# Gate and up projections of four feed-forward blocks computed with seven block products for eight (Strassen's scheme in Winograd's form)

## The chip, the core and the metric

The kernel runs on one core of one Trainium2 chip. The metric is device time in microseconds (us). A profiled execution gives the trace; its span is a little shorter than the device time of the same run.

## What is computed

The trunk has two layers on a sequence of 512 frames with a model width of 1024. Each layer is a feed-forward block, a token mixer (layer 0 a hybrid of two attentions, layer 1 a latent attention) and a second feed-forward block; so there are four feed-forward blocks of the same shape, cut from the reference here:

```python
def _swiglu(u, w_gate, w_up, w_down):          # 1024 -> 2816 -> 1024
    return (jax.nn.silu(u @ w_gate) * (u @ w_up)) @ w_down
# per layer, with shift, scale and gate from cond @ ada_w[i] (1024 x 9*1024) + ada_b[i]
u = _rmsnorm(h, norm_g[i, 0]) * (1 + sc1) + sh1
h = h + 0.5 * g1 * _swiglu(u, w_gate[i, 0], w_up[i, 0], w_down[i, 0])
u = _rmsnorm(h, norm_g[i, 1]) * (1 + sc2) + sh2
h = h + g2 * mixer(u)
u = _rmsnorm(h, norm_g[i, 2]) * (1 + sc3) + sh3
h = h + 0.5 * g3 * _swiglu(u, w_gate[i, 1], w_up[i, 1], w_down[i, 1])
```

Everything is float32.

## The kernel before

**Products.** The model dimension lies on 8 blocks (k) of 128 partitions, the 2816 hidden features on 22 tiles (j) of 128; the 512 frames are the columns. A float32 operand is split into a high part and a rest (`split`, L348; for weights `wsplit`, L262), and one float32 product is three matmuls with the smaller types, high by high, high by rest, rest by high (`mm3`, L297, the matmuls on L299 to L301). A weight chunk (`wchunk`) is a DMA of 512 KB into a `raw` buffer, a copy on ACT into `wh` (L265) and a subtraction on DVE into `wl` (L266, operands `raw` and `wh`, both in SBUF). There are two `raw` buffers and four each of `wh` and `wl`.

**A feed-forward block** (`ffn`, L542). For a hidden tile j, `unit` runs 8 x 3 matmuls of 512 columns for the gate and as many for up, into two PSUM tiles (`pj`, `s`); `gated` applies Silu on ACT, multiplies on DVE (L557, one operand in PSUM) and splits the product (L349 on ACT, L350 on DVE). In the three later blocks the first two tiles are computed in two halves of 256 columns, so that they can begin while the normalised input of the second half is still made (`affine`, L411: L413 reads `h` in SBUF and a PSUM tile, L418 two SBUF tiles). The first block has `first_feed` instead, which feeds tiles 0 to 2 block by block of k while its input arrives. After all 22 tiles `back_proj` computes the down projection, 8 x 22 x 3 matmuls, and adds into `h` (L441, in `Back.tile`).

**Work in the background.** The shift, scale and gate vectors need the product of the conditioning vector with `ada_w`. It is cut into items (`ada_chunk`, L182): a DMA of 512 KB into one of two `wide` buffers (L185, from SP) and one DVE instruction over 128 x 1024 that sums along the free axis (L186, both inputs in SBUF). They lie in the list `pending`; `background(n)` issues n of them, and `need` issues one after another until the vector asked for is there.

**Order.** The instructions of each engine are put in order when the kernel is built; each engine runs its list strictly in that order and waits for semaphores of others. GpSimd (POOL) has work in the hybrid mixer only: weight subtractions, rotary products (L656 to L658) and MEMSETs.

The places that the change touches are `ffn`, `u_next` (L604), `affine` and `apply`, `turn_x` of the first feed, and the loop over the layers.

Of the kernel before, what the change touches and what calls it, by code (L numbers as in the profile page):

```python
# [16 lines left out]
P = 128  # L17
NT = 5
NRAW = 2
# [77 lines left out]
def kernel(ctx: ExitStack, tc: tile.TileContext, d):  # L97
# [84 lines left out]

    def ada_chunk(l, j, k, raw=None):
# [62 lines left out]
    def wload(ap, n):  # L246
        raw = wp.tile([P, 1024], F32, tag="raw", name=nm("raw"), bufs=NRAW)
        nc.sync.dma_start(raw[:, :n], ap)
        return raw
# [161 lines left out]
    def affine(src, rb, k, a, b, oh, ol):  # L411
        t = t_tile()[:, :src.shape[-1]]
# [10 lines left out]
    def apply(srcs, rb, c0, c1, a, b, outs):  # L423
        w = c1 - c0
        for k, (src, (oh, ol)) in enumerate(zip(srcs, outs)):
            affine(src[:, c0:c1], rb[:, :w], k, a, b, oh[:, c0:c1], ol[:, c0:c1])
# [115 lines left out]
    def ffn(l, f, u, gate, nxt, feed=None, rate=2, after=None):  # L542
# [22 lines left out]

        if feed is not None:
# [9 lines left out]
            for j in range(3):  # L576
                gated(j, *pss[j], 0, T)
        else:
            j0 = 2
            first = [load(0), load(1)]  # L580
            for c0, c1 in HALVES:
# [3 lines left out]
                for j in range(2):  # L585
                    pss = pj_ps(), s_ps()
                    run_tiles([ps[:, :w] for ps in pss], first[j], u, c0, c1)
                    gated(j, *pss, c0, c1)
        for j in range(j0, NF):
            unit(j, *load(j), 0, T)  # L590
            background(rate)
            if after is not None and j == after[0]:
                after[1]()

        def down(k):
            out = []
            for c, (k0, k1) in enumerate(((0, 8), (8, 16), (16, 22))):
                wh, wl = wchunk(d["wd"][l, f, k][:, k0 * P:k1 * P], (k1 - k0) * P)
                out.append((wh, wl, k1 - k0))
            return out  # L600

        back_proj(gate(), down, hidden, nxt, 1)

    def u_next(l, sub):  # L604
        outs = [(u_tile(), u_tile()) for _ in range(KD)]

        def nxt(acc, c0, c1):
# [8 lines left out]
            def two():  # L616
                with tc.high_priority(offset=PRIO), tc.issue_after(last_mm[0]):
                    rb = spread(dg[0], c1 - c0)
                apply(h_tiles(), rb, c0, c1, acol[l, sub], bcol[l, sub], outs)
            later(HOLD1, one)  # L620
            later(HOLD2, two)
        return outs, nxt
# [580 lines left out]
    def first_ada(k):  # L1203
        for i, j in enumerate((1, 0)):
            n = 2 * k + i
            with tc.issue_after(last_y[0]) if last_y[0] is not None else nullcontext():
                ada_chunk(0, j, k, None if n % 3 == 2 else spare[(n - n // 3) % 4])
# [19 lines left out]
    turned = []  # L1227
# [8 lines left out]
    def first_feed(k):  # L1236
# [8 lines left out]
        t = t_tile()  # L1245
        S.activation(t, turned[k], AF.Identity, scale=acol[0, 0][:, k:k + 1], bias=bcol[0, 0][:, k:k + 1])
        split(*u[k], t)
        if k + 2 < KD:
# [4 lines left out]
    pending.extend(ada_work(0, [("g", 0), ("n", 1), ("g", 1), ("n", 2), ("g", 2)]))  # L1253
# [13 lines left out]

    for l in range(2):
        n_u, n_nxt = u_next(l, 1)
        ffn(l, 0, u, need(gcol, (l, 0)), n_nxt, first_feed if l == 0 else None, 3,  # L1270
# [119 lines left out]
```

## Time and profile before

| | before |
|---|---|
| device time, median of 3 runs | 2006.46 us (2005.85 to 2012.56) |
| device time of the profiled run | 2006.17 us |
| its span | 2004.4 us |
| granted TensorE clock, mean over the span | 0.995 |
| PE busy (matmul) | 1956.1 us, 98% of the span |
| DVE / ACT / POOL busy | 1094.6 / 744.7 / 120.4 us |

"Busy" is the time in which an engine has an instruction in work. Successive matmuls overlap, so their distance is read from starts, not from durations. A granted clock of 1.00 is 2.4 GHz, 0.50 is 1.2 GHz.

### The profile page before, as it was taken

How to read it: one execution, taken by the hardware profiler on the slowest of the kernel's cores; microseconds unless marked ns; L12 is line 12 of the kernel's file. 1: busy time of each engine (PE TensorE's matmuls, PEld its weight loads, DVE VectorE, ACT ScalarE, POOL GpSimd, SP SyncE). 2: the span in 40 equal slices, each digit the busy share in tenths (PEclk: the TensorE clock that was granted, in tenths of full speed). 3: DMA queues.
4: the chain of work that ended last, by engine and by line, in shares of the span. 5: the costliest groups of instructions: out<-in, count | busy, mean ns of one | idle time of the engine just before them, and what ended most of it. 6: DMA issues, size and time to landing. Idle time of an engine off the chain costs nothing.

```text
span 2004.4 us, 25366 instructions
## 1 busy us (share of the span) xinstructions
PE 1956.1 (98%) x9988; PEld 1652.8 (82%) x9988; DVE 1094.6 (55%) x1893; ACT 744.7 (37%) x1232; POOL 120.4 (6%) x116
## 2 busy tenths in 40 slices
PE   7999999999989999999999999999999999999997
PEld 4888888987878888888889888888988898888886
DVE  7466673479946577777336433323586573333234
ACT  6322222246667442222224233222357543232221
POOL 0000000045553000000000000000000000000000
PEclk9999999999999999999999999999999999999998
DMA  9467773232222238887432333233232023322331
GB/s 334 135 228 241 236 234 105 92 107 67 85 79 80 85 121 270 280 274 248 117 97 85 107 99 95 92 98 97 71 99 71 23 94 109 103 95 95 95 97 61
DMA packets 78412, 260.53 MB, mean 130 GB/s; under 512 B 9426, under 2 KB 12498, under 8 KB 78292
## 3 DMA queue, kind: packets, MB, share of 16 engines
q1 hardware_dynamic: 75892, 254.65, 39.5%
q0 software_dynamic: 1664, 3.28, 0.7%
q8 instruction: 78, 1.28, 0.3%
q10 hardware_dynamic: 736, 0.98, 0.2%
q14 instruction: 42, 0.34, 0.1%
HBM read 249.17 MB, written 2.10 MB: 125 GB/s over the span
## 4 chain that ended last, share of the span: by engine, by line
PE 83%; DVE 10%; ACT 3%; DMA 2%; issue 1%; POOL 1%; SPq 0%; DVEq 0%; ACTq 0%; POOLq 0%
PE pj L299 18%; PE pj L301 18%; PE pj L300 18%; PE s L301 9%; PE s L300 9%; PE s L299 9%; DVE hid L978 1%; DVE m L977 1%; DVE wl L266 1%; DVE hid L767 1%; DVE hid L350 1%; DVE sm L699 1%; PE aux L718 1%; ACT wide L707 1%; ACT wh L265 1%
## 5 line engine op out<-in xcount | busy, mean ns | idle before, releaser
L265 ACT ACTIVATE wh<-raw 128x1024 fp32r<-128x1024 f32 (+1 forms) x331 | 340.8, 1030 | 899.6 <-PE pj L300 561.9
L266 DVE TENSOR_TENSOR wl<-raw,wh 128x1024 fp32r<-128x1024 f32 (+2 forms) x308 | 364.6, 1184 | 417.5 <-ACT wh L265 417.0
L299 PE MATMUL pj<-u,wh 128*128 128x512 f32 (+1 forms) x1035 | 391.1, 379 | 2.0 <-ACT u L349 0.9
L301 PE MATMUL pj<-u,wl 128*128 128x512 f32 (+1 forms) x1035 | 382.5, 370 | 0.7 <-DVE wl L266 0.5
L300 PE MATMUL pj<-u,wh 128*128 128x512 f32 (+1 forms) x1035 | 381.4, 370 | 0.8 <-DVE u L350 0.8
L299 PE MATMUL pj<-hid,wh 128*128 128x512 f32 (+1 forms) x876 | 319.5, 365 | 0.2 <-DVE h L441 0.2
L300 PE MATMUL pj<-hid,wh 128*128 128x512 f32 (+1 forms) x876 | 317.2, 362 | 0.0
L301 PE MATMUL pj<-hid,wl 128*128 128x512 f32 (+1 forms) x876 | 317.2, 362 | 0.0
L301 PE MATMUL s<-u,wl 128*128 128x512 f32 (+1 forms) x841 | 311.3, 370 | 0.0
L300 PE MATMUL s<-u,wh 128*128 128x512 f32 (+1 forms) x841 | 310.8, 370 | 0.0
L299 PE MATMUL s<-u,wh 128*128 128x512 f32 (+1 forms) x841 | 310.6, 370 | 0.0
L299 PEld LDWEIGHTS pj<-u,wh 128*128 128x128 f32 x1035 | 196.3, 190 | 35.6 <-issue 3.1
L301 PEld LDWEIGHTS pj<-u,wl 128*128 128x128 f32 x1035 | 195.5, 189 | 34.4 <-DVE wl L266 1.5
L300 PEld LDWEIGHTS pj<-u,wh 128*128 128x128 f32 x1035 | 195.6, 189 | 31.2 <-DVE u L350 1.9
L186 DVE SCALAR_TENSOR_TENSOR wide<-wide,cond 128x1024 f32<-128x1024 f32 x133 | 161.3, 1223 | 73.4 <-DMA wide<-in_ada 73.2
L299 PEld LDWEIGHTS pj<-hid,wh 128*128 128x128 f32 x876 | 165.5, 189 | 25.8 <-DVE hid L770 0.4
L301 PEld LDWEIGHTS pj<-hid,wl 128*128 128x128 f32 x876 | 165.3, 189 | 25.4
L300 PEld LDWEIGHTS pj<-hid,wh 128*128 128x128 f32 x876 | 165.4, 189 | 24.9
L301 PEld LDWEIGHTS s<-u,wl 128*128 128x128 f32 x841 | 158.8, 189 | 26.8
L300 PEld LDWEIGHTS s<-u,wh 128*128 128x128 f32 x841 | 158.6, 189 | 26.5
L299 PEld LDWEIGHTS s<-u,wh 128*128 128x128 f32 x841 | 158.5, 189 | 26.0
L557 DVE TENSOR_TENSOR t<-t,s 128x512 f32<-128x512 f32 (+1 forms) x93 | 60.5, 651 | 162.8 <-PE s L301 159.5
(214 smaller groups left out, 1920.2 us busy)
## 6 DMA issues: line engine op xcount, KB each, us to landing
raw<-in_wgu SPq DMA_DIRECT2D x176, 512.0 KB, 3.5
wide<-in_ada SPq DMA_DIRECT2D x133, 512.0 KB, 4.4
raw<-in_wd SPq DMA_DIRECT2D x64, 512.0 KB, 3.5
raw<-in_wd SPq DMA_DIRECT2D x32, 384.0 KB, 3.1
raw<-in_hin SPq DMA_DIRECT2D x19, 512.0 KB, 3.5
h<-in_ada SPq DMA_DIRECT2D x11, 512.0 KB, 7.1
raw<-in_hv SPq DMA_DIRECT2D x8, 512.0 KB, 3.5
raw<-in_hout SPq DMA_DIRECT2D x8, 512.0 KB, 3.6
```

Of the source, the lines that this page charges most:

```text
L186: V.scalar_tensor_tensor(raw, raw, 1.0, cond[0], op0=ALU.mult, op1=ALU.mult, accum_out=mod[l][:, j, k:k + 1])
L265: S.activation(wh[:, :n], raw[:, :n], AF.Copy)
L266: (by or V).tensor_tensor(wl[:, :n], raw[:, :n], wh[:, :n].bitcast(F32), op=ALU.subtract)
L299: PE.matmul(ps, ah, bh, start=start, stop=False)
L300: PE.matmul(ps, ah, bl, start=False, stop=False)
L301: last_mm[0] = PE.matmul(ps, al, bh, start=False, stop=stop).ins
L350: return V.tensor_tensor(ol, raw, oh.bitcast(F32), op=ALU.subtract)
L557: V.tensor_tensor(sg[:, :w], sg[:, :w], pu[:, :w], op=ALU.mult)
L699: V.tensor_reduce(nmx, ps[:, :n], axis=AX.X, op=ALU.max, negate=True)
L707: S.activation(pr[qt], pr[qt], AF.Copy, scale=rinv[:, qt:qt + 1])
L718: last_mm[0] = PE.transpose(ps[:, c:c + P], pr[qt][:, kt * P:(kt + 1) * P], ident).ins
L767: V.tensor_tensor(ol, ps, oh.bitcast(F32), op=ALU.subtract)
```

## The change

Two neighbouring hidden tiles are taken as a pair. Their weights are a 2 x 2 arrangement of blocks (two halves of the model dimension by two hidden tiles), and so is the input (two halves of the model dimension by two halves of the frames); four 128-row blocks each stand in a half. For each of gate and up, seven products of 4 x 3 matmuls of 256 columns are made (84 matmuls; the two units that a pair replaces have 48 matmuls of 512 columns for each of gate and up). The products use sums of weight blocks and of input blocks, and their results are recombined. Tiles that stay in the old form: the first four of the first block, the first two of the others. That leaves 9 + 10 + 10 + 10 = 39 pairs, 78 sets of seven products.

- `Forms` holds one set of weights and goes in six steps: four loads of 256 KB; four sums on POOL (L586 to L589, 128 x 512 each); three splits of 1024 columns and one of 512 (ACT L268, DVE L269). `pair_products` calls the steps for the next sets at fixed places between the products of the present one.
- Recombination per set: ACT copies two PSUM halves, DVE adds (L642, L648, L654: one operand in SBUF, one in PSUM), POOL adds 128 x 256 (L649). Per pair: two Silu on ACT, two products on POOL (L696, 128 x 512), four hidden splits of 256 columns (ACT L352, DVE L353).
- Input sums: `input_sums` makes, for each of four pairs of input blocks, four POOL instructions of 256 columns (L559 to L562) and two splits of 512. In the three later blocks the normalised tile is kept without its shift (`kept`), and a POOL TENSOR_SCALAR of 512 columns for each of eight tiles (L782) adds the shift first.
- The down projection is made in three parts after hidden tiles 6, 14 and 22; the first two parts add into `h` by L752, the last runs through `back_proj`. The sets of the next part are brought up to their first splits during the last four k of a part.
- Background: one item for each pair, two for each k of the first two parts; `need` for the gate vector comes after the first part's pairs, no longer after the last tile. `raw` gets four buffers.

```diff
-NRAW = 2
+NRAW = 4
+    def input_sums(t1, t2):
+        lo, hi = slice(0, HALF), slice(HALF, T)
+        G.tensor_tensor(t1[:, lo], t1[:, hi], t1[:, lo], op=ALU.subtract)
+        G.tensor_tensor(t1[:, hi], t1[:, hi], t2[:, hi], op=ALU.add)
+        G.tensor_tensor(t2[:, hi], t2[:, hi], t1[:, lo], op=ALU.add)
+        G.tensor_tensor(t2[:, lo], t2[:, lo], t2[:, hi], op=ALU.subtract)
+        out = []
+        for t in (t1, t2):
+            o = hid_tile(), hid_tile()
+            split(*o, t)
...
+    class Forms:
...
+        def load(self):
+            self.r.append(raw_tile())
+            self.a2 = hid_tile(F32), hid_tile(F32)
+            for i, o in enumerate((self.r[0][:, :T], self.r[0][:, T:], *self.a2)):
+                nc.sync.dma_start(o, self.ap[i])
+
+        def sums(self):
...
+            G.tensor_tensor(s3, a21, a11, op=ALU.subtract)
+            G.tensor_tensor(s2, a22, s3, op=ALU.subtract)
+            G.tensor_tensor(s1, a21, a22, op=ALU.subtract)
+            G.tensor_tensor(s4, a12, s2, op=ALU.subtract)
+
+        def split(self):
+            n = len(self.w)
+            self.w.append(wsplit(self.r[n], 2 * T) if n < 3 else wsplit(self.a2[1], T))
...
+    def pair_products(w, u, sums, nxt):
...
+        ahead(0, 2)
+        w.to(6)
...
+        product(b1[:, lo], "A11", block(0, lo))
+        S.activation(t[:, lo], b1[:, lo], AF.Copy)
+        product(b26[:, lo], "A12", block(1, lo))
+        ahead(0, 3)
+        product(b26[:, hi], "S2", lambda q: sums[q][1])
+        V.tensor_tensor(two(ca), twice(t[:, lo]), two(b26), op=ALU.add)
+        product(b57[:, lo], "S1", lambda q: sums[q][0])
+        ahead(0, 4)
+        ahead(1, 1)
+        product(b57[:, hi], "S3", lambda q: sums[q][2])
+        S.activation(t[:, hi], b57[:, lo], AF.Copy)
+        V.tensor_tensor(two(cb), twice(ca[:, hi]), two(b57), op=ALU.add)
+        G.tensor_tensor(ca[:, hi], cb[:, hi], t[:, hi], op=ALU.add)
+        product(b34[:, lo], "S4", block(1, hi))
+        ahead(0, 5)
+        product(b34[:, hi], "A22", lambda q: sums[q][3])
+        ahead(0, 6)
+        V.tensor_tensor(cb, cb, b34, op=ALU.add)
+        return ca, cb
+    PARTS = ((0, 6), (6, 14), (14, 22))
...
+            for x in g:
+                S.activation(x, x, AF.Silu)
+            left[0] -= 1
+            p = products()
+            for x, y in zip(p, g):
+                G.tensor_tensor(x, x, y, op=ALU.mult)
...
-        for j in range(j0, NF):
-            unit(j, *load(j), 0, T)
-            background(rate)
...
+            g = gate()
+            if p1 < NF:
+                for k in range(KD):
+                    ps = pj_ps()
+                    run_tile(ps, down(k), act, 0, T)
+                    mark[0] = V.scalar_tensor_tensor(h[:, k], ps, g[:, k:k + 1], h[:, k],
+                                                     op0=ALU.mult, op1=ALU.add).ins
+                    background(rate[1])
+                    if k >= KD - 4:
+                        forms[0].to((1, 2, 3, 4)[k - KD + 4])
+            else:
+                back_proj(g, down, act, nxt, 3)
...
+                if keep and c1 == T:
+                    for q in range(KD // 2):
+                        for k in (2 * q, 2 * q + 1):
+                            G.tensor_scalar(kept[k], kept[k], bcol[l, sub][:, k:k + 1], None, op0=ALU.add)
+                        sums.append(input_sums(kept[2 * q], kept[2 * q + 1]))
```

The first place to look at is a pair in the middle of a part. On DVE, of the changed kernel, from the second set of one pair to the first set of the next (in the first block; `wl` are weight splits, `s` and `aux` PSUM tiles, `wide` a background item):

```order
L269 TENSOR_TENSOR wl_1977<-raw_1881,wh_1976 128x1024 [waits DMAHW6_49,DMAHW7_49,PE_49,Activation_49]
L642 TENSOR_TENSOR hid_1948<-t_1950,s_1945 128x512 [waits PE_49]
L269 TENSOR_TENSOR wl_2006<-raw_1938,wh_2005 128x1024 [waits PE_49,Activation_49]
L648 TENSOR_TENSOR hid_1949<-hid_1948,aux_1946 128x512 [waits DVE_49,Activation_49]
L654 TENSOR_TENSOR hid_1949<-hid_1949,aux_1947 128x512 [waits PE_49,Pool_49]
L269 TENSOR_TENSOR wl_2060<-hid_1883,wh_2059 128x512 [waits DMAHW2_49,Activation_49]
L353 TENSOR_TENSOR hid_2067<-hid_1948,hid_2066 128x256 [waits Pool_49]
L353 TENSOR_TENSOR hid_2073<-hid_1948,hid_2072 128x256 [waits DMAHW0_49,Activation_49]
L189 SCALAR_TENSOR_TENSOR wide_2078,mod_92<-wide_2078,cond_94 128x1024
L269 TENSOR_TENSOR wl_2120<-raw_2009,wh_2119 128x1024 [waits DMAHW3_49,DMAHW4_49,PE_49,Activation_49]
```

The splits of the pair's hidden tiles wait for POOL's products, and behind them on DVE stands the first weight split of the next pair's second set. On POOL, which had nothing in a feed-forward block, the same pair in the changed kernel reads:

```order
L586 TENSOR_TENSOR raw_2082<-hid_2010,raw_2009 128x512
L587 TENSOR_TENSOR raw_2081<-hid_2011,raw_2082 128x512
L649 TENSOR_TENSOR hid_1948<-hid_1949,t_1950 128x256
L588 TENSOR_TENSOR raw_2081<-hid_2010,hid_2011 128x512
L696 TENSOR_TENSOR hid_1948<-hid_1948,hid_1820 128x512
L589 TENSOR_TENSOR raw_2082<-raw_2009,raw_2081 128x512
L696 TENSOR_TENSOR hid_1949<-hid_1949,hid_1821 128x512
```

The sums for the set after the next stand ahead of and between the products on which the hidden splits wait.

The second place is the entry of a later feed-forward block (here the second of layer 0), on POOL of the changed kernel; `hid_7601` to `hid_7608` are the kept tiles, `raw_7943` and `raw_7944` hold the sums of the block's first set:

```order
L782 TENSOR_SCALAR hid_7601<-hid_7601,b_2_3707 128x512
L559 TENSOR_TENSOR hid_7601<-hid_7601 128x256
L560 TENSOR_TENSOR hid_7601<-hid_7601,hid_7602 128x256
L561 TENSOR_TENSOR hid_7602<-hid_7602,hid_7601 128x256
L562 TENSOR_TENSOR hid_7602<-hid_7602 128x256
L561 TENSOR_TENSOR hid_7608<-hid_7608,hid_7607 128x256
L562 TENSOR_TENSOR hid_7608<-hid_7608 128x256
L586 TENSOR_TENSOR raw_7944<-hid_7937,raw_7936 128x512
L587 TENSOR_TENSOR raw_7943<-hid_7938,raw_7944 128x512
```

All 24 instructions on the input stand ahead of the first weight sum; the third product of the first pair needs both.

The third place is the down projection of the first part in the first block, on DVE, where before a hidden tile of a unit stood between background items:

```order
L186 SCALAR_TENSOR_TENSOR wide_838,mod_92<-wide_838,cond_94 128x1024
L186 SCALAR_TENSOR_TENSOR wide_841,mod_92<-wide_841,cond_94 128x1024
L266 TENSOR_TENSOR wl_1009<-raw_1006,wh_1008 128x1024
L557 TENSOR_TENSOR t_909<-t_909,s_884 128x512
L350 TENSOR_TENSOR hid_913<-t_909,hid_912 128x512
```

In the changed kernel, from the last items before the gate vector `g_0` to the third k:

```order
L189 SCALAR_TENSOR_TENSOR wide_962,mod_92<-wide_962,cond_94 128x1024 [waits DMAHW6_49,DVE_49]
L189 SCALAR_TENSOR_TENSOR wide_965,mod_92<-wide_965,cond_94 128x1024 [waits DMAHW7_49,DVE_49]
L211 TENSOR_TENSOR g_0_968<-mod_92,vec 128x8 [waits DVE_49]
L213 TENSOR_SCALAR g_0_968<-g_0_968 128x8 [waits DVE_49]
L752 SCALAR_TENSOR_TENSOR h<-pj_971,g_0_968,h 128x512 [waits DVE_49]
L189 SCALAR_TENSOR_TENSOR wide_997,mod_92<-wide_997,cond_94 128x1024 [waits DMAHW0_49]
L752 SCALAR_TENSOR_TENSOR h<-pj_1003,g_0_968,h 128x512
L189 SCALAR_TENSOR_TENSOR wide_1000,mod_92<-wide_1000,cond_94 128x1024 [waits DMAHW1_49]
L189 SCALAR_TENSOR_TENSOR wide_1029,mod_92<-wide_1029,cond_94 128x1024 [waits DMAHW2_49,DVE_49]
L752 SCALAR_TENSOR_TENSOR h<-pj_1035,g_0_968,h 128x512 [waits PE_49]
```

Eight items stand ahead of `g_0`, and each L752 frees one of the two PSUM tiles `pj` for a later k only after the items in front of it.

## Rows read from the trace of the kernel before

**Rows 1.** The page, busy time of each engine (share of the span), instructions.
```profile
PE 1956.1 (98%) x9988; PEld 1652.8 (82%) x9988; DVE 1094.6 (55%) x1893; ACT 744.7 (37%) x1232; POOL 120.4 (6%) x116
```
**Rows 2.** The page, the chain that ended last, by engine.
```profile
PE 83%; DVE 10%; ACT 3%; DMA 2%; issue 1%; POOL 1%; SPq 0%; DVEq 0%; ACTq 0%; POOLq 0%
```
**Rows 3.** Window inside a feed-forward block: engines' busy time, clock, DMA share, GB/s.
```profile
1100.00:1320.00 220.00, 220.00 (x973) 182.16 (x972) 82.39 (x93) 64.47 (x83) 0.00 (x0) 1.00 0.31 98
```
**Rows 4.** Timeline, PE, 512 columns: start, duration, instruction; 46 steps apart.
```profile
1109.64 0.39 PE L300 MATMUL s<-u,wh 128*128 128x512 f32 x1
...
1120.07 0.39 PE L301 MATMUL pj<-u,wl 128*128 128x512 f32 x1
```
**Rows 5.** Timeline, PE, 256 columns; 83 steps apart.
```profile
372.46 0.28 PE L299 MATMUL pj<-hid,wh 128*128 128x256 f32 x1
...
382.41 0.28 PE L301 MATMUL pj<-hid,wl 128*128 128x256 f32 x1
```
**Rows 6.** Groups by line, weight loads of that stretch: busy, mean ns.
```profile
L299 PEld LDWEIGHTS pj<-hid,wh 128*128 128x128 f32 x28 | 5.4, 192 | 0.0
```
**Rows 7.** Groups by line and form: busy us, mean ns, idle before.
```profile
L266 DVE TENSOR_TENSOR wl<-raw,wh 128x1024 fp32r<-128x1024 f32 x268 | 328.0, 1224 | 306.9 <-ACT wh L265 306.4
L266 POOL TENSOR_TENSOR wl<-raw,wh 128x1024 fp32r<-128x1024 f32 x23 | 56.0, 2439 | 96.7 <-ACT wh L265 90.3 <-PE aux L718 6.4
L871 POOL MEMSET hid<- 64x512 f32 x8 | 4.3, 539 | 0.4
```
**Rows 8.** Timeline, POOL, two products of 512 columns in a row.
```profile
534.89 1.29 POOL L656 TENSOR_TENSOR hid<-hid,rope 128x512 f32<-128x512 f32 x1
536.13 1.29 POOL L657 TENSOR_TENSOR hid<-hid,rope 128x512 f32<-128x512 f32 x1
```
**Rows 9.** Timeline, DVE and POOL at the same time in the hybrid mixer.
```profile
417.47 3.25 DVE L350 TENSOR_TENSOR hid<-hid,hid 64x512 fp32r<-64x512 f32 x1
417.79 2.38 POOL L266 TENSOR_TENSOR wl<-raw,wh 128x1024 fp32r<-128x1024 f32 x1
...
423.74 2.92 POOL L266 TENSOR_TENSOR wl<-raw,wh 128x1024 fp32r<-128x1024 f32 x1 [3.57 <-ACT wh L265]
423.77 0.68 DVE L658 TENSOR_TENSOR hid<-hid,t 128x512 f32<-128x512 f32 x1
...
431.50 2.40 POOL L266 TENSOR_TENSOR wl<-raw,wh 128x1024 fp32r<-128x1024 f32 x1 [0.35 <-ACT wh L265]
431.57 2.37 DVE L941 TENSOR_TENSOR hid<-hid 128x32 f32<-128x32 f32 x1
```
**Rows 10.** Timeline, DVE beside POOL, one operand of DVE in PSUM.
```profile
497.38 4.74 POOL L266 TENSOR_TENSOR wl<-raw,wh 128x1024 fp32r<-128x1024 f32 x2 [9.21 <-ACT wh L265]
...
499.70 0.68 DVE L767 TENSOR_TENSOR hid<-pj,hid 128x512 fp32r<-128x512 f32 x1
```
**Rows 11.** Windows after a wait of PE, columns as in rows 3.
```profile
588.00:592.00 4.00, 1.30 (x5) 1.14 (x6) 3.25 (x6) 3.55 (x7) 1.85 (x3) 0.50 0.30 68
592.00:596.00 4.00, 4.00 (x14) 3.04 (x13) 0.85 (x2) 0.77 (x3) 3.21 (x3) 0.71 0.46 168
```
**Rows 12.** Timeline, PE, the end of that wait.
```profile
590.70 0.55 PE L294 MATMUL s<-hid,hid 128*128 128x256 f32 x1 [5.46 <-DMA hid<-hid]
```
**Rows 13.** Timeline, entry of a feed-forward block, DVE.
```profile
1079.48 0.48 DVE L413 SCALAR_TENSOR_TENSOR t<-h,a,aux 128x256 f32<-128x256 f32 x1 [0.34 <-PE aux L403]
...
1086.06 0.47 DVE L418 SCALAR_TENSOR_TENSOR u<-t,b,u 128x256 fp32r<-128x256 f32 x1
```
**Rows 14.** Timeline, same entry, PE: the first matmul of 512 columns.
```profile
1093.07 0.40 PE L299 MATMUL pj<-u,wh 128*128 128x512 f32 x1
```
**Rows 15.** Timeline, DVE: the first two and the 71st of 72 background items.
```profile
742.39 1.22 DVE L186 SCALAR_TENSOR_TENSOR wide<-wide,cond 128x1024 f32<-128x1024 f32 x1
...
743.53 1.22 DVE L186 SCALAR_TENSOR_TENSOR wide<-wide,cond 128x1024 f32<-128x1024 f32 x1
...
944.77 1.23 DVE L186 SCALAR_TENSOR_TENSOR wide<-wide,cond 128x1024 f32<-128x1024 f32 x1 [1.61 <-DMA wide<-in_ada]
```

More of the change, by code (lines that the diff above doesn't have):

```diff
@@ L181, with raw_tile @@
     mark = [None]
+    def raw_tile():
+        return wp.tile([P, 1024], F32, tag="raw", name=nm("raw"), bufs=NRAW)
     def ada_chunk(l, j, k, raw=None):
@@ L246, in wload @@
     def wload(ap, n):
-        raw = wp.tile([P, 1024], F32, tag="raw", name=nm("raw"), bufs=NRAW)
+        raw = raw_tile()
         nc.sync.dma_start(raw[:, :n], ap)
@@ L540, in first_products @@
             mm3(ps, wh[:, sl], wl[:, sl], *u[k], k == 0, k == KD - 1)
-    def ffn(l, f, u, gate, nxt, feed=None, rate=2, after=None):
+    HALF = T // 2
+    def input_sums(t1, t2):
[8 more added lines that the diff above has]
+            split(*o, t)
+            out += [tuple(x[:, c] for x in o) for c in (lo, hi)]
+        return [out[0], out[3], out[1], out[2]]
@@ L543, in ffn @@
+    PARTS = ((0, 6), (6, 14), (14, 22))
+    def ffn(l, f, u, sums, gate, nxt, feed=None, rate=(2, 2), after=None):
         hidden = []
@@ L577, in ffn @@
                 gated(j, *pss[j], 0, T)
+            forms[0].to(2)
+            unit(j0, *load(j0), 0, T)
+            j0 = 4
         else:
@@ L585, in ffn @@
                 for j in range(2):
+                    if c0:
+                        forms[0].to(2 + 2 * j)
                     pss = pj_ps(), s_ps()
@@ L588, in ffn, with down, u_next @@
                     gated(j, *pss, c0, c1)
-        for j in range(j0, NF):
-            unit(j, *load(j), 0, T)
-            background(rate)
[L592 to L604, printed above, removed]
+        for p0, p1 in PARTS:
+            js = range(max(j0, p0), p1, 2)
+            left[0] = 2 * len(js)
+            for j in js:
+                pair(j)
+            if after is not None and p1 == NF:
+                after()
+            act = hidden[p0:p1]
+            def down(k):
+                return [(*wchunk(d["wd"][l, f, k][:, p0 * P:p1 * P], (p1 - p0) * P), p1 - p0)]
+            g = gate()
[10 more added lines that the diff above has]
+                back_proj(g, down, act, nxt, 3)
+    def u_next(l, sub, keep=False):
         outs = [(u_tile(), u_tile()) for _ in range(KD)]
+        kept, sums = [], []
         def nxt(acc, c0, c1):
@@ L1292, in final @@
                     nc.sync.dma_start(d["out"][:, 4 * g:4 * g + 4, c0:c1], o)
-            ffn(1, 1, u, need(gcol, (1, 2)), final)
+            ffn(1, 1, *x, need(gcol, (1, 2)), final)
 def _consts():
```

100 lines of the change are left out of this document (80 added, 20 removed).

## The prediction

> **What bounds the kernel now.** I read the page first: matmuls are in work for 98% of the span, DVE for 55%, POOL for 6% [rows 1]. The chain of waits gives the same order, 83% on PE [rows 2]. Then the windows: inside a feed-forward block PE is busy for the whole of 220 us at full clock, while DVE is busy 37% of it and POOL not at all [rows 3]. So the time of these blocks is the number of matmuls times their pitch. The timeline of PE gives the pitch: 46 steps of 512 columns in 10.43 us, 0.2267 each [rows 4]; 83 steps of 256 columns in 9.95 us, 0.120 each [rows 5]. Two of the half-width matmuls cost 6% more than one of full width.
>
> **Matmuls.** A set (gate or up of a pair) was 48 x 0.2267 = 10.88 us and becomes 84 x 0.120 = 10.08 us. That is 0.80 less, not the eighth that the count of products suggests. For 78 sets: **-62.4 us**. A pair goes from 21.76 to 20.16 us. The down projection has the same matmuls as before, and the pieces of it are priced at nothing in PE time.
>
> **The pairs.** What decides is whether 20.16 us hide the work of the other engines. Two things there are new to a feed-forward block: POOL is used, and DVE's operands lie in SBUF. In the timeline of the hybrid mixer the two engines stop each other. A DVE instruction over 64 x 512 with two operands in SBUF takes 3.25 us and ends when POOL's instruction beside it has ended; one of 32 columns takes 2.37 us beside POOL's 2.40; and POOL's takes 2.92 instead of 2.40 where DVE had begun first [rows 9]. With one operand in PSUM, DVE's instruction takes 0.68 us in the middle of POOL's work [rows 10]. So DVE's instructions with two SBUF operands and POOL's instructions use one thing in turn, each for the whole of an instruction; I call it the port.
>
> Port work of one pair:
> - POOL: eight sums and two products of 512 columns and two adds of 256. Two products in a row start 1.24 us apart and take 1.29 [rows 8]; I take 1.27. For 256 columns a line through this and the 2.44 of 1024 columns [rows 7] gives about 0.68. 10 x 1.27 + 2 x 0.68 = 14.1 us.
> - DVE with two SBUF operands: six weight splits of 1024 columns, two of 512 and four hidden splits of 256. Instructions of 1024 in a row start 1.14 us apart [rows 15], and the mean duration of a split is 1.22 [rows 7]. With 1.14, and 0.6 and 0.35 by columns: 6 x 1.14 + 2 x 0.6 + 4 x 0.35 = 9.4 us. A background item, where one is left, adds 1.14.
> - Sum 23.5 us, or 24.7 with an item: more than the 20.16 of the matmuls, and more than the 21.76 of before.
> - DVE's six recombinations with a PSUM operand, 6 x 0.6 = 3.6 us, run beside POOL. If all fell where POOL is idle, the pair would be 27.1 to 28.3 us. POOL works some 57% of the pair, so I let 1.5 of the 3.6 stand alone: 24.1 + 1.5 = **25.6 us**, 5.4 over the matmuls. The order supports that this isn't hidden: behind POOL's products stand the hidden splits on DVE, and behind these the next set's first weight split.
>
> The first set of a part has its sums and splits (4 x 1.27 + 4.0 = 9.1 us) under the down projection of the part before. Two pairs at a part's start are therefore 2 x 25.6 - 9.1 = 42.1 us against 40.3, 1.8 late. In 12 parts there are 39 pairs, so 27 passages from a pair to the next: 11 first ones at 1.8 and 16 others at 5.4: **+106 us**. Bounds: 16 at 3.3 (port alone) and nothing for the first, 53; all serial, 16 x 8.1 + 11 x 4 = 174.
>
> **The clock.** After PE had waited 5.46 us [rows 12], the next two windows show granted clocks of 0.50 and 0.71 [rows 11]: 6 to 7 us at 1.2 GHz, which costs half of that, 3.4 us. In a pair the 5.4 us of waiting fall in several pieces, so I take about a third of that, 1.25, for each of the 16 passages: **+20** (0 to 27).
>
> **The entry of the three later blocks.** Take T0 as the first normalised tile of the second half. Before, PE has its two halved tiles done and begins at full width at T0+13.6 [rows 13, 14]. The third product of the first pair (S2, after two of 12 x 0.12) is due at T0+16.4. Its weights pass POOL behind all 24 instructions on the input. Eight TENSOR_SCALARs of 512: the trace has none on POOL; its nearest rows are a MEMSET of 512 on half the partitions, 0.54 [rows 7], and the two-input product, 1.27. I take 0.9, the middle. 8 x 0.9 + 16 x 0.68 + 3 x 1.27 = 21.9 us. DVE's own port work in that time (eight additions in the normalisation [rows 13], eight splits of 512 of the sums, weight and hidden splits) is about 10 us and takes turns with it. With the first tile's 0.9 and the split on ACT and DVE behind the sum, S2 is ready at about T0+35.7: 19.3 us late, three times 58, between 49 and 67 by the two prices of the TENSOR_SCALAR. Each such wait costs the 3.4 of the clock besides: **+68 us** (59 to 77). The Trainium skill, page "GPSIMD Engine Reference", section "4.1 Engine selection", says that one-input operations there run at about the rate of its lanes; an estimate by that page, 512 columns at 1.2 GHz or 0.43 us, would make each entry 3.8 us shorter, 11 in all, and no row of this case shows it.
>
> **The gate vector and the background items.** Before, `need` for the gate came after 22 tiles, with all items long done. Now it comes after the first part, and two items are issued with each k of the down projection; each adds into `h` behind them on DVE, and frees the PSUM tile that a later k waits for. A run of items goes at 2.89 us each (70 steps in 202.4 us), held by its DMA, although DVE needs 1.14 [rows 15]. In the first block 16 such items lie between the first part's last pair and the sixth addition, and the first product of the next pair waits for a tile freed there: 16 x 2.89 + 3.7 = 50 us where the part's down projection (8 x 18 x 0.2267) takes 32.6: 17 to 20 late. In the second block of layer 0, 15 items: 14 to 17. In layer 1 the items are fewer than the k can carry or used up: nothing. Together 34, with the clock twice: **+41 us** (30 to 45).
>
> **The rest.** The first feed gains 16 POOL instructions of 256 and eight splits of 512, 16 x 0.68 + 8 x 0.6 = 15.7 us of port work; the last quarter of it, 3.9, can't be hidden: +5 (0 to 10). Ends of the parts, where hidden splits wait for POOL: +3 (0 to 10). The mixers get four `raw` buffers; I cost that at nothing, covered by their matmuls (-5 to 5).
>
> **Sum.** -62 + 106 + 20 + 68 + 41 + 5 + 3 = +181 us. On the profiled run's 2006.2 us that is 2187, and the run lies 0.3 below the median shown; I take **2185 us**. With all low ends -62 + 53 + 59 + 30 - 5 = +75, 2081; with all high ends 2292.
>
> **Rivals.**
> 1. *Matmuls alone.* Everything new hides under PE: 2006 - 62 = 1944 us. For it: DVE is free 63% of the time in these blocks [rows 3]. Against: 23.5 us of port work in 20.16. It ends on the other side, and the point from which it decides is a port pair under 20.2 us, that is POOL's 512 columns at 0.9 us or less. Chance 0.06.
> 2. *No port, only queues.* If DVE and POOL ran freely, DVE would need 14 and POOL 14 us for a pair, and pairs would hide. What stays is POOL's list at the entry (9.3 late, 28 for three), the items (41) and some 8 of the rest: 2006 - 62 + 77 = 2021; with easier entries it comes to no change. Against: each overlap in [rows 9]. Chance 0.07.
> 3. *The port stays with one side.* DVE's instruction that found POOL at work waited for all of it, and POOL's 2.92 came after two DVE instructions in a row [rows 9]. If the waiting side loses several turns, a pair is all serial, 28.3 us, and PE waits long enough for the low clock in each: the high end, 2280. Chance 0.17.
> 4. *Weight loads set the pitch.* A load takes 192 ns [rows 6], as the matmul of 256 columns now comes every 120. If loads didn't overlap each other, a set would be 84 x 0.192 = 16.1 us, 5.2 more than before: +409 for 78 sets, 2415 us, with the port's work hidden under it. Against: the pitch of 0.120 was measured with those loads [rows 5]. Chance 0.02. The page "TensorE: Matmul & The Clock Gate" of the Trainium skill, section "Back-to-back issue gap", says that load and matmul together set the spacing of a stream; at this width the trace shows a spacing by columns alone (0.120 for 256, 0.2267 for 512).
>
> **Chances.** Forecast 0.68. Its own range is 2120 to 2245, the bounds of the pairs' and the entries' terms taken not all to one side. Rival 3 lies above, rival 2 below; 2070 to 2280 leaves out rival 1, rival 4 and part of 2 and 3. Within 0.5% (about what can be told from no change here) is 1996 to 2016: rival 2 with cheap entries, 0.03. Faster: rival 1, 0.06. Slower: 0.91.
>
> **What would show it.** In the timeline after: POOL's sums longer than 1.29 us or DVE's splits longer than 1.22 where they overlap; pairs 25 us apart in a part's middle, with PE's longest waits on `wl` L269 and behind L353. In the second, third and fourth block PE waits 15 to 22 us before the third product of the first pair, released by DVE `wl` behind POOL L782 and L559 to L562. In the first part's down projection of both blocks of layer 0, PE waits for L752 behind L189. If pairs stand 20 us apart, the port's term is wrong; if PE is idle nowhere in the entry, the entry's.

## Result, and the profile after

The changed kernel takes 2257.98 us (median of 4 runs, 2254.0 to 2264.77) against 2007.36 us of the kernel before: ratio 1.1247, 95% interval 1.1209 to 1.1285. 2185 us was predicted, with 2120 to 2245 as the forecast's own range and 2070 to 2280 as the wider one, which takes in part of rivals 2 and 3; the result lies in the wider one only. The profiled run's span is 2262.8 us.

The first part of the page after, to be held against [rows 1]:

```profile
PE 2016.5 (89%) x12813; PEld 1816.9 (80%) x12820; DVE 1571.1 (69%) x2395; ACT 941.5 (42%) x1662; POOL 919.9 (41%) x672
```

POOL now works 919.9 us, and no engine fills the span: PE has lost nine points of its share. The durations say why. Groups by line and form of the kernel after, busy us and mean ns of one, idle time before:

```profile
L269 DVE TENSOR_TENSOR wl<-raw,wh 128x1024 fp32r<-128x1024 f32 x346 | 489.4, 1415 | 106.4 <-ACT wh L268 104.1
L353 DVE TENSOR_TENSOR hid<-hid,hid 128x256 fp32r<-128x256 f32 x156 | 93.3, 649 | 14.3 <-ACT hid L352 14.3
L586 POOL TENSOR_TENSOR raw<-hid,raw 128x512 f32<-128x512 f32 x78 | 121.1, 1552 | 355.8 <-DVE wl L269 218.2 <-DMA hid<-in_wgs 67.1 <-DMA wide<-in_ada 38.6
L649 POOL TENSOR_TENSOR hid<-hid,t 128x256 f32<-128x256 f32 x78 | 113.2, 1452 | 221.0 <-DVE hid L648 203.1 <-DMA hid<-in_wgs 17.9
L642 DVE TENSOR_TENSOR hid<-t,s 128x512 f32<-128x512 f32 x78 | 52.9, 678 | 0.0
L782 POOL TENSOR_SCALAR hid<-hid,b 128x512 f32<-128x512 f32 x24 | 45.5, 1901 | 402.0 <-DVE u L421 402.0
```

A weight split takes 1415 ns on average where it took 1224 [rows 7], and POOL's sum of 512 columns 1552 where two in a row took 1290 [rows 8]; POOL's add of 256 columns takes 1452, twice its price. L642, with one operand in PSUM, stays at 678. The timeline of the two engines inside a pair shows the turns:

```profile
379.11 1.71 DVE L269 TENSOR_TENSOR wl<-raw,wh 128x1024 fp32r<-128x1024 f32 x1
379.82 2.17 POOL L586 TENSOR_TENSOR raw<-hid,raw 128x512 f32<-128x512 f32 x1
380.75 0.67 DVE L648 TENSOR_TENSOR hid<-hid,aux 128x512 f32<-128x512 f32 x1
381.34 1.72 DVE L269 TENSOR_TENSOR wl<-raw,wh 128x1024 fp32r<-128x1024 f32 x1
382.07 2.15 POOL L587 TENSOR_TENSOR raw<-hid,raw 128x512 f32<-128x512 f32 x1
```

The split that starts at 379.11 ends at 380.82. POOL's sum starts at 379.82 and ends at 381.99, 1.17 us after that, about what it takes alone; DVE's L648 runs through in 0.67 in the middle of it, and the split of 381.34 again waits for the sum's end. The last three passages of a part of four pairs, a window with the columns of [rows 3]:

```profile
2129.40:2203.60 74.20, 67.38 (x495) 64.68 (x494) 52.22 (x55) 31.67 (x54) 41.63 (x31) 0.93 0.32 98
```

Three pairs take 74.2 us where their matmuls need 60.5 at full clock.

The entry of layer 0's second block: the first normalised tile of the second half, POOL's list, and the third product on PE.

```profile
786.02 0.48 DVE L416 SCALAR_TENSOR_TENSOR hid<-h,a,aux 128x256 f32<-128x256 f32 x1 [0.51 <-PE aux L406]
...
787.84 1.57 POOL L782 TENSOR_SCALAR hid<-hid,b 128x512 f32<-128x512 f32 x1 [84.94 <-DVE u L421]
...
814.21 0.80 POOL L562 TENSOR_TENSOR hid<-hid 128x256 f32<-128x256 f32 x1
814.97 1.71 POOL L586 TENSOR_TENSOR raw<-hid,raw 128x512 f32<-128x512 f32 x1
816.76 1.59 POOL L587 TENSOR_TENSOR raw<-hid,raw 128x512 f32<-128x512 f32 x1
...
820.89 0.58 PE L302 MATMUL s<-hid,wh 128*128 128x256 f32 x1 [6.15 <-ACT wh L268]
```

S2 begins 34.9 us after T0 = 786.02; T0+35.7 was predicted. Here and in the next block's entry POOL passes without a pause from the first shift to the weight sums. The first part's down projection in the first block, last items before two of the additions into `h`, and the waits of PE there:

```profile
130.36 1.23 DVE L189 SCALAR_TENSOR_TENSOR wide<-wide,cond 128x1024 f32<-128x1024 f32 x1 [1.55 <-DMA wide<-in_ada]
132.04 0.75 DVE L752 SCALAR_TENSOR_TENSOR h<-pj,g,h 128x512 f32<-128x512 f32 x1
...
158.44 2.26 DVE L189 SCALAR_TENSOR_TENSOR wide<-wide,cond 128x1024 f32<-128x1024 f32 x1 [0.24 <-DMA wide<-in_ada]
160.63 0.74 DVE L752 SCALAR_TENSOR_TENSOR h<-pj,g,h 128x512 f32<-128x512 f32 x1
```

```profile
PE pj L302 <- DVE h L752: 17.7, 2, 16.8
```

PE waits 16.8 us for the first addition, which stands behind eight items, and begins the next pair only after the one at 160.63 has ended, 53.6 us after the last addition of the pair before (107.8); 50 was predicted.

By the last write into `h` of each block, the four feed-forward blocks are 67, 77, 65 and 48 us longer than before, in order of time, and the two mixers together 3.

### The profile page after: what moved, and what is told of

Its sections match the earlier page's. It is cut to its first block, busy times and chain, and to the rows that moved or that the text cites. A ratio compares the mean times of both kernels' runs of the same rounds, so it can differ in the third digit from the quotient of the medians.

```text
span 2262.8 us, 33583 instructions
## 1 busy us (share of the span) xinstructions
PE 2016.5 (89%) x12813; PEld 1816.9 (80%) x12820; DVE 1571.1 (69%) x2395; ACT 941.5 (42%) x1662; POOL 919.9 (41%) x672
## 5 line engine op out<-in xcount | busy, mean ns | idle before, releaser
L269 DVE TENSOR_TENSOR wl<-raw,wh 128x1024 fp32r<-128x1024 f32 (+2 forms) x386 | 530.3, 1375 | 119.9 <-ACT wh L268 117.4
L268 ACT ACTIVATE wh<-raw 128x1024 fp32r<-128x1024 f32 (+2 forms) x409 | 415.0, 1028 | 441.2 <-PE pj L303 283.3
L302 PE MATMUL pj<-u,wh 128*128 128x256 f32 (+1 forms) x723 | 251.4, 349 | 58.5 <-ACT wh L268 44.4
L304 PE MATMUL pj<-u,wl 128*128 128x256 f32 (+1 forms) x723 | 244.5, 338 | 35.1 <-DVE wl L269 35.0
L586 POOL TENSOR_TENSOR raw<-hid,raw 128x512 f32<-128x512 f32 x78 | 121.1, 1552 | 355.8 <-DVE wl L269 218.2
L303 PE MATMUL pj<-u,wh 128*128 128x256 f32 (+1 forms) x723 | 238.6, 331 | 3.9 <-DVE u L353 2.5
L304 PE MATMUL aux<-hid,wl 128*128 128x256 f32 x780 | 222.7, 286 | 3.6 <-DVE wl L269 3.6
L352 ACT ACTIVATE hid<-hid 128x256 fp32r<-128x256 f32 (+2 forms) x192 | 81.9, 450 | 344.1 <-POOL hid L696 267.7
L302 PE MATMUL aux<-hid,wh 128*128 128x256 f32 x780 | 222.4, 285 | 0.0
L303 PE MATMUL aux<-hid,wh 128*128 128x256 f32 x780 | 222.3, 285 | 0.0
L302 PE MATMUL s<-u,wh 128*128 128x256 f32 (+1 forms) x685 | 212.7, 311 | 0.6 <-ACT wh L268 0.6
L303 PE MATMUL s<-u,wh 128*128 128x256 f32 (+1 forms) x685 | 211.3, 309 | 0.0
L302 PEld LDWEIGHTS pj<-u,wh 128*128 128x128 f32 x723 | 148.1, 205 | 77.6 <-ACT wh L268 51.4
L304 PE MATMUL s<-u,wl 128*128 128x256 f32 (+1 forms) x685 | 210.0, 307 | 0.0
L782 POOL TENSOR_SCALAR hid<-hid,b 128x512 f32<-128x512 f32 x24 | 45.5, 1901 | 402.0 <-DVE u L421 402.0
L649 POOL TENSOR_TENSOR hid<-hid,t 128x256 f32<-128x256 f32 x78 | 113.2, 1452 | 221.0 <-DVE hid L648 203.1
```

The lines of the kernel that those rows point to most:

```text
L268: S.activation(wh[:, :n], raw[:, :n], AF.Copy)
L269: (by or V).tensor_tensor(wl[:, :n], raw[:, :n], wh[:, :n].bitcast(F32), op=ALU.subtract)
L302: PE.matmul(ps, ah, bh, start=start, stop=False)
L303: PE.matmul(ps, ah, bl, start=False, stop=False)
L304: last_mm[0] = PE.matmul(ps, al, bh, start=False, stop=stop).ins
L352: S.activation(oh, raw, AF.Copy)
```

## Experiments

The measure of the pairs in all of them is the time from the end of the first to the end of the last pair in a part of four: 60.5 us of matmuls at full clock. The changed kernel has 71.8 to 76.5, mean 73.9, over its eight such parts.

**Unread sums.** POOL works, and no split waits for a sum.

```diff
-            self.w.append(wsplit(self.r[n], 2 * T) if n < 3 else wsplit(self.a2[1], T))
+            self.w.append(wsplit(self.r[0], 2 * T) if n < 3 else wsplit(self.a2[1], T))
```

> The changed kernel, but the weight splits read the loaded first tile in place of the sums; POOL still makes every sum, and nobody waits for it (the products are therefore of other weights). Theory of the shared port: POOL's work stays, so the pairs in the middle of a part stay near 24.8 us (layer 0) and 26.2 us (layer 1), and the time near 2230 to 2255 us, some us won at the entries. Rival, that the pairs are late through the chain from a sum to its split and not through the port: the pairs fall to 20.2 to 21 us and the time to about 2140 us.

Measured 2302.45 us (1.1462, 1.1392 to 1.1532). The parts take 74.0 us on average, as in the changed kernel:

```profile
2170.50:2245.30 74.80, 67.02 (x494) 63.71 (x493) 49.09 (x55) 31.56 (x54) 44.64 (x31) 0.95 0.29 96
```

So in the pairs the chain from a sum to its split holds nothing up. That the kernel became 44 us slower, about half of it at the first down projections of layer 0 (94 and 90 us from pair to pair for 84 and 79), was not foreseen and was not followed up.

**No sums.** The same, and `sums` does nothing.

> The same, and the weight sums on POOL are left out altogether (the splits read the loaded first tile). Theory of the shared port: port work of a pair falls from 23.5 to 13.4 us, under the 20.2 of the matmuls, so the pairs go to 20.2 to 20.7 us; 111 us of lateness in the pairs go and some 20 at the entries and ends of parts: about 2110 us. The difference to the kernel with unread sums is then the price of the port alone, over 100 us. Rival, that the chain and not the port holds the pairs: the time is the same as with unread sums, within 20 us.

Measured 2130.85 us (1.0608, 1.0547 to 1.0668); parts 63.4 us:

```profile
2001.80:2063.60 61.80, 61.60 (x496) 60.40 (x494) 43.14 (x53) 30.71 (x50) 17.22 (x12) 1.00 0.32 99
```

In this stretch PE is busy throughout at full clock. Nobody read the sums of the run before, and without them 172 us are gone. Between the two kernels there is, besides the port, a coupling by buffers: POOL's sum waits for a `raw` buffer that DVE's split frees (218.2 us of idle before L586 in the table above).

**Loose sums.** POOL makes four differences of loaded blocks for each set into tiles that nobody reads, so that neither data nor buffers tie the sums to DVE.

```diff
+            for x, y in ((a21, a11), (a22, a11), (a21, a22), (a12, a22)):
+                G.tensor_tensor(hid_tile(F32), x, y, op=ALU.subtract)
```

> The changed kernel with unread sums, now with POOL's four sums per set written to tiles of their own that no engine reads, each from loaded blocks alone, so that POOL's sums wait for DVE no more and DVE for them no more, neither by data nor by buffers; the products are of other weights. What is left between the two engines beside the adds and products of before is the port. Theory of the port: the pairs stay well over those of the kernel without sums (22.2 and 21.6 us), 23.5 us or more, and the time is 2200 us or more. Rival, that a ring of buffer waits (POOL for raw buffers that DVE's splits free, ACT and DVE for POOL) made the 24.8 to 26.2 us: pairs at 21.5 to 22.5 us as without sums, the time near 2130 to 2150 us.

Measured 2287.99 us (1.1396, 1.1363 to 1.1429), parts 76.5 us. The ring of buffers is not the cause. In its timeline the sums reach into the hidden splits:

```profile
2152.00 1.86 DVE L353 TENSOR_TENSOR hid<-hid,hid 128x256 fp32r<-128x256 f32 x2
2153.54 2.91 POOL L586 TENSOR_TENSOR hid<-hid,raw 128x512 f32<-128x512 f32 x2
2154.05 2.68 DVE L353 TENSOR_TENSOR hid<-hid,hid 128x256 fp32r<-128x256 f32 x2 [0.20 <-ACT hid L352]
2156.42 1.48 POOL L586 TENSOR_TENSOR hid<-hid,hid 128x512 f32<-128x512 f32 x1
2156.66 2.32 DVE L269 TENSOR_TENSOR wl<-raw,wh 128x1024 fp32r<-128x1024 f32 x1
```

Two hidden splits take 2.68 us where they take 0.4 each alone, and a weight split 2.32.

In the loose kernel POOL's sums still stand in POOL's list ahead of its adds and products, so the place in that list is a rival to the port. The same stretch of this kernel and of the one without sums decides between them:

```profile
2152.10:2225.90 73.80, 63.83 (x478) 61.98 (x478) 56.26 (x53) 30.25 (x50) 49.71 (x32) 0.93 0.25 79
```

DVE's 53 instructions are in work for 56.26 us here and for 43.14 without the sums, 13.1 more, and the stretch is 12.0 us longer. DVE's idle time does not grow (17.5 us here, 18.7 there), and it waits 0.6 us for POOL in both. So what the sums cost here is the lengthening of DVE's own instructions beside them.

**Everything on DVE.** Sums, adds, products, input sums and shift.

```diff
-            G.tensor_tensor(s3, a21, a11, op=ALU.subtract)
+            V.tensor_tensor(s3, a21, a11, op=ALU.subtract)
...
-                            G.tensor_scalar(kept[k], kept[k], bcol[l, sub][:, k:k + 1], None, op0=ALU.add)
+                            V.tensor_scalar(kept[k], kept[k], bcol[l, sub][:, k:k + 1], None, op0=ALU.add)
```

> The changed kernel with every instruction that the change gave to POOL put on DVE (sums, products, adds, input sums, shift); the same values. Theory of the port: nothing is excluded any more; DVE has 12 x 0.6 + 4 x 0.35 + 9.4 + 3.6 minus what it shares, about 19.7 us a pair (20.9 with a background item) against 20.2 of PE, so pairs take 20.5 to 21.5 us; the entries shorten by 8 to 12 us each, since 256 columns take 0.35 there and not 0.70: 2090 to 2130 us. Rival, that more work on one in-order engine makes DVE the bound: pairs stay at 24 us or more and the time above 2220 us.

Measured 2060.88 us (1.0259, 1.0224 to 1.0295): better than expected, with parts of 59.5 us.

```profile
1943.50:2003.10 59.60, 59.60 (x493) 59.30 (x492) 56.31 (x86) 34.98 (x55) 0.00 (x0) 1.00 0.41 124
```

DVE works 94% of this window and PE the whole of it at full clock. In this kernel's groups a weight split is back at the price of [rows 7]:

```profile
L269 DVE TENSOR_TENSOR wl<-raw,wh 128x1024 fp32r<-128x1024 f32 x346 | 421.4, 1220 | 55.1 <-ACT wh L268 52.6
```

An engine that took on more work ended each of its instructions sooner, and 197 us of the 251 that the change lost came back. A second effect, not separated from the first, is in this number: DVE does a sum in 0.68 us, POOL in 1.29.

```profile
L587 DVE TENSOR_TENSOR raw<-hid,raw 128x512 f32<-128x512 f32 x78 | 53.4, 685 | 0.3
```

**No input sums.**

```diff
-            first_sums.append(input_sums(*first_t[-2:]))
-                            G.tensor_scalar(kept[k], kept[k], bcol[l, sub][:, k:k + 1], None, op0=ALU.add)
-                        sums.append(input_sums(kept[2 * q], kept[2 * q + 1]))
```

> The changed kernel without input sums: no kept tiles, no shift and no sums of input blocks on POOL and no splits of them; the products take plain input blocks in their place. Theory: S2 of the first pair is no longer late by 18 us in each of three blocks, nor is the clock low behind it: 3 x 26 us less, and 5 to 13 in the first feed, about 2170 us. Rival, that the entry waits for the first sets' own loads, sums and splits: at most 25 us less, 2235 us.

Measured 2205.01 us (1.0977, 1.0929 to 1.1024), 53 less and not 88. The stretches with the entries of layer 1 fall by 18 and 16 us (128.7 to 111.0 and 310.1 to 294.6 from pair to pair), that of the hybrid mixer and the entry behind it by 20, the first feed by 7.5. The 18 for S2 are confirmed. The rest of the entry's loss stays; by elimination it belongs to the first sets' own sums and splits, and in one entry this is seen: in layer 1's first block PE waits 7.0 us for the normalisation, where two small DVE instructions (L385, L387, 128 x 2, both operands in SBUF) take 1.21 and 1.19 us beside POOL's L587 and L588, 0.16 each otherwise, and the weight split ahead of them 2.20.

**No background items.**

```diff
+        if raw is None:
+            return
         nc.sync.dma_start(raw, d["ada"][l, j * KD + k])
```

> The changed kernel without the background items (neither their DMA nor their DVE instruction; the shift, scale and gate vectors are of other values, those of the first normalisation excepted). Theory: the first part's down projection no longer waits for items; the 32, 26, 13 and 5 us that lie between its last pair and the next one beyond the 52.8 us of matmuls shrink to 5 to 8 each, and the pairs of layer 1 go from 26.2 to 24.8 us: about 2180 us (2165 to 2195). Rival, that these waits come from the hidden splits behind POOL and from the weight loads: at most 25 us less, 2235 us, most of it in the pairs of layer 1.

Measured 2191.78 us (1.0899, 1.0871 to 1.0927), 66 less. From the first part's last pair to the next one it is 55.7, 58.8, 55.8 and 57.8 us instead of 84.3, 78.8, 65.6 and 57.8: the items cost 28.6 + 20.0 + 9.8 there. The pairs did not do what was expected: those of layer 1 stay at 74.8 us, those of layer 0 go up from 73.1 to 74.8. An item between two pairs costs nothing there, and parts without items are the longer ones; the reason was not tried.

**Filled waits.** Matmuls whose results are overwritten are put where PE waits.

```diff
+    def fill(u, o, n):
+        for _ in range(n):
+            PE.matmul(o, u[0][0][:, :P], u[0][0][:, :HALF], start=True, stop=True)
...
+        fill(u, b57[:, lo], filled[0] * 36)
         product(b1[:, lo], "A11", block(0, lo))
...
+        fill(u, b57[:, lo], filled[0] * 50)
         product(b26[:, hi], "S2", lambda q: sums[q][1])
...
+                    if k == 2 and p0 == 0 and l == 0:
+                        fill(u, aux_ps()[:, :HALF], 120)
```

> The changed kernel with matmuls of 256 columns into a PSUM region that is overwritten later, placed where PE waits: 36 before the first and 50 before the third product of the first pair in the three later blocks, 120 before the third k of the first part's down projection in layer 0. They keep PE at work in waits of 4.5, 6.2 and 16.8 us, so that the clock should stay at full level there. Theory, that in these stretches the chain of POOL, DVE and the items' DMA sets the time and the low clock costs PE little: at most 15 us less than the changed kernel. Rival, that the low clock is paid in full: 10 us at each entry and 8.5 at each of two down projections, some 40 to 47 us less, about 2215 us.

Measured 2266.2 us (1.1291, 1.127 to 1.131): nothing won. Windows of the same two stretches (an entry with its first pair; the first block's first down projection with the pair behind it), first in the changed kernel, then in this one:

```profile
773.60:846.60 73.00, 59.39 (x415) 56.42 (x416) 51.57 (x78) 29.52 (x52) 54.02 (x41) 0.86 0.13 43
107.80:192.20 84.40, 62.57 (x352) 54.18 (x351) 70.36 (x89) 17.78 (x25) 31.61 (x18) 0.88 0.64 214
```

```profile
769.80:842.80 73.00, 67.15 (x510) 64.28 (x511) 50.20 (x78) 29.46 (x52) 53.64 (x41) 0.95 0.14 43
108.90:191.00 82.10, 74.73 (x479) 67.78 (x477) 67.50 (x89) 18.86 (x28) 30.96 (x18) 0.98 0.68 220
```

The mean clock rises from 0.86 to 0.95 and from 0.88 to 0.98, and the stretches take 73.0 and 82.1 us instead of 73.0 and 84.4. The fills did not hold up real work: behind them PE still waits 0.2 us (first product), 1.9 us (third product) and 2.9 us (third k). PE at half speed was still not what the others waited for. In the pairs of a part's middle no fill was tried.

**First part in the old form**, the change's engines.

```diff
-        j1 = 4 if feed is not None else 2
+        j1 = 6
...
+        for j in range(j0, j1):
+            unit(j, *load(j), 0, T)
+            background(rate[2])
```

> The changed kernel, but the first six hidden tiles of each block are in the old form (32 pairs in place of 39), with 4 items behind each of these tiles in layer 0 and 2 in layer 1; the engines stay as in the change. Theory: the entry's work on POOL and the items now lie beside matmuls of 512 columns that don't wait for them; 81 us of the entries and some 55 of the 75 us at the first down projections go, 7 x 1.6 = 11 us of matmuls come back, the pairs of parts 2 and 3 stay at 24.8 to 26.2: about 2130 us. Rival, that the same port work meets the first tiles' weight splits and makes these late: 2180 us or more.

Measured 2190.15 us (1.0891, 1.0867 to 1.0915), 60 over the expectation and in the rival's range. Parts stay at 73.7 us. By the writes into `h` the blocks won 9, 21, 24 and 19 us. The entries did not become free: in the first 45 us of the three later blocks PE is idle for 7.4, 11.0 and 5.6 us, in the first two of them 4.5 of it at a time for a weight's copy. The rival's cause fits, but nothing separated it from the rest.

**The same with DVE in POOL's place**, once with the input sums and the shift left on POOL, once with all on DVE:

> First six hidden tiles in the old form, weight sums, adds and products of the pairs on DVE, the input sums and the shift on POOL. If the port and the places of the entry and of the items are the whole of what the change lost, this keeps most of the 64 x 0.8 = 51 us of matmuls: 1965 to 1990 us, faster than the kernel before. Rival, that DVE at 20 to 21 us a pair is itself the bound and part ends cost some us each: 2000 to 2020 us, no change. Rival, that input sums on POOL delay DVE's weight splits at the entry: 5 to 10 us more at each of three entries.

> The same with the input sums and the shift on DVE too. They are 8 + 16 instructions of DVE, some 10 us in each entry, in an engine that in the old form is busy 37 to 60% there; they are needed only 43 us later. Expected the same as with POOL within 10 us: 1965 to 1995 us. If the scheduler puts them ahead of weight splits that PE waits for, 2000 us or more.

Measured 2052.49 us (1.0203, 1.0186 to 1.022) and 2048.52 us (1.0185, 1.0163 to 1.0206). Both expected times fell; the second lies where the scheduler's branch (2000 us or more) had put it. The parts are at the matmuls' limit (59.6 us), so the loss lies ahead of the first pairs; in the second kernel's first block:

```profile
119.51 0.80 PE L302 MATMUL pj<-hid,wh 128*128 128x512 f32 x1 [13.90 <-DVE h L751]
```

The addition still waits for items: of the twelve that had gone out before it, eight were the loads of `h`, which stand first in the list. In layer 1's second block, the stretch from the mixer's end to the first pair takes 132.6 us with 6.5 of PE idle and a mean clock of 0.97:

```profile
1672.40:1805.00 132.60, 126.12 (x727) 110.68 (x726) 85.64 (x152) 49.49 (x76) 0.00 (x0) 0.97 0.26 80
```

**Input sums later, items earlier**, all on DVE, first six tiles in the old form.

```diff
+                    def summed(q):
+                        for k in (2 * q, 2 * q + 1):
+                            S.activation(kept[k], kept[k], AF.Identity, bias=bcol[l, sub][:, k:k + 1])
+                        sums[q] = input_sums(kept[2 * q], kept[2 * q + 1])
...
             unit(j, *load(j), 0, T)
             background(rate[2])
+            for q in [todo.pop(0) for _ in range(-(-len(todo) // (j1 - j)))]:
+                sums[q]()
```

> As the kernel with the first six tiles in the old form and all new work on DVE, but the input sums are made behind units 2 to 5 and not in the entry, the shift of the kept tiles is added by ACT, and the items go 6 (first block), 3 or 2 behind each unit, one for each k of the first part. Expected: the wait of 13.9 us before the first block's third k and the 5 to 12 us of waiting and low clock at the entries go: 2048 less 35, 2005 to 2020 us; the remaining distance to the 1955 of the matmuls alone is in the first feed, the hybrid mixer and part ends. If the items only move their waits to the units, 2035 us or more.

Measured 1999.36 us (median of 8; 0.9953, 0.9937 to 0.9968): faster than the kernel before, by half a per cent. The stretch of the window above:

```profile
1628.90:1752.10 123.20, 123.16 (x727) 109.76 (x726) 82.45 (x144) 53.62 (x84) 0.00 (x0) 1.00 0.28 87
```

Nine us less, PE never idle, full clock. By the writes into `h`, the last block now takes 13 us less than in the kernel before, which is its 16 sets at 0.80; the first block takes 8 more, the second and third 5 and 2 less, so most of their gain is still lost elsewhere.

## Why the prediction was right, and where its sum was off

The direction, the main mechanism and its places were right; the sum was 73 us short. Term by term, predicted against measured by stage (the clock's 37 us, predicted as a term of its own, stand in a row):

| term | predicted | measured |
|---|---|---|
| matmuls | -62 | -62 (PE full in 59.6 us for 493 matmuls when nothing holds it) |
| pairs | +106 | 8 x (73.9 - 60.5) = 107, and 4 in the three parts of two |
| low clock | +37 | no cost of its own where it was tried |
| three entries | +58 | 26 + 30 + 25 = 81 |
| first down projections | +34 | 32 + 26 + 13 + 5 = 76 |
| other ends of parts | +3 | 24 before the last parts, 17 to 19 in them |
| first feed | +5 | 13, what the first block has left over; not measured by itself |

The sum of the measured column is about 260; the spans differ by 258. The first feed's term is a remainder, so the sum is no test of the first block.

**Pairs.** 25.6 us a pair, or 73.1 for three passages behind a first one, was forecast; 73.9 was measured. That the totals meet so closely is partly luck. The forecast made a part's first passage short (1.8 us late) and the others long (5.4 late, 25.6). Measured, first passages take 24.5 to 26.5 us, middle ones 24.8 to 26.2, and the last ones 21.9 to 24.8: the short one is the last, in whose second set nothing is prepared for a next one. The mechanism is the port. With the sums unread the three passages take 74.0, untied 76.5, left out 63.4; and with DVE's idle time equal, DVE's longer instructions alone make up the difference between the last two in the stretch shown above. In the changed kernel's stretch DVE is idle for 22 and POOL for 33 of 74.2 us, so the port is not always taken. Against the 61.8 us without sums DVE is in work 9.1 us longer and idle 3.3 us longer: turns account for most of it, waits that follow from the fixed order of the lists for the rest. The step "a background item adds 1.14" was wrong, since the parts without items are the longer ones.

**Low clock.** The failed step is "costs half of that, 3.4 us", and with it the 20 us in the pairs and the 3.4 behind every stall. The granted clock did fall as forecast (0.945 over the span), but at the entry and at the first down projection the stretches are set by POOL, DVE and DMA: with PE kept at work they took 73.0 and 82.1 us for 73.0 and 84.4. For the pairs it was not tried. A clock term was due only where PE was next on the chain.

**Entry.** S2 came 34.9 us after T0 instead of 35.7, and two errors met there. The TENSOR_SCALAR of 512 columns took 1.57 us where nothing held it up (1.90 on average), above both bounds (0.54 and 1.27), and DVE's port work beside the list was less than 10 us: POOL's list took 31.9 us from the first shift to the third weight sum, for 28.0 of undisturbed instructions. The Trainium skill's page "GPSIMD Engine Reference", section "4.1 Engine selection", puts one-input operations at roughly line rate, worked out as an estimate of 0.43 us in the prediction; this trace does not agree with it. The sign named for the entry, a wait of 15 to 22 us before the third product, was not seen as such: PE waits 4.5 us before the first product and 6.1 before the third, and works at a granted clock of 0.50 to 0.75 in between. The first product needs no sum, but on ACT the copy of its weights stands behind copies of the input sums, which wait for POOL (L560). What was left out is the pair behind: the second set's sums (up to 2.3 us each in turn with splits) make it some 7 us longer.

**Items.** The pace was right (18 items in the first block start 2.79 us apart; 2.89 was forecast), and so, nearly, was the instant at which PE came free, 53.6 us for 50. But it came from another addition: PE waited for the seventh, behind 18 items, where the forecast had the sixth behind 16. Two things were missing: after the stall the next pair is late as well (in the first block 31 us from there to its end, for 20.2 of matmuls), and the third block, priced at nothing, lost 13 us: two items for each k need 5.8 us where a k has 4.1. Without items the four stretches are 55.7 to 58.8 us.

**Ends of parts** were priced at 3 us and took some 42. Part of this is hidden splits waiting for POOL's products; over all twelve ends PE waits 24.5 us for their copies:

```profile
PE pj L302 <- ACT hid L352: 24.5, 12, 3.1
```

Whether the rest comes from the next part's first sums was not taken apart. With everything on DVE the stretch between two parts of four is 64.7 us in layer 1, for 63.7 of matmuls. This, the items and the entries are the terms that made the forecast low.

Rivals: "no port" fell with the loose sums, "the port stays with one side" had the time nearly right (2280) but not the pairs (28.3 us a pair, for 24.8 to 26.2 in a part's middle), "matmuls alone" describes what DVE alone reaches in the pairs, and weight loads do not bind: 493 half-width matmuls in 59.6 us are 0.121 each, with a load before each.

## What to carry to other kernels

Before work is given to GpSimd, add up, for the stage, its time and that of VectorE's instructions with two SBUF operands: the two take turns, and here the sum (some 24 us by estimate, 24.8 to 26.2 measured) and not the larger of the two set the pace; the same work on VectorE alone hid under 20.2 us of matmuls. Saved matmuls count only where the new sums, splits and waits fit under those that remain: of 51 us in the best version 9 were kept. And a low clock is a symptom until it is shown that TensorE is next on the chain.

## What the hardware showed that was not expected

- A one-input TENSOR_SCALAR of 128 x 512 in float32 on GpSimd took 1.57 us, more than the two-input TENSOR_TENSOR's 1.29.
- Half clock cost nothing where another engine set the time: a mean clock of 0.86 raised to 0.95 left 73.0 us at 73.0.
- A VectorE instruction of 128 x 2 with two SBUF operands took 1.21 us beside GpSimd's sums for 0.16 otherwise, as part of a wait of 7.0 us that TensorE had for a normalisation.
